# Two layers of a two-block transformer kernel: experts in pairs on float32 weights, four state-space states at a time

## The chip, the cores and the metric

The kernel runs on one core of one Trainium2 chip, as one launch. The metric is the device time of one execution in microseconds; lower is better. Three runs of the kernel before gave 2289.42, 2290.0 and 2290.57 us, so their median is 2290.0 us.

## The reference

The work is a forward pass over 256 tokens of width 1024, all in float32. It has two blocks. Block one has two layers (adaLN, a conformer convolution beside a Mamba-2 scan, then a mixture of experts). Block two has four layers: forgetting attention ("fox"), a state space layer ("S5"), a pooling mixer, and fox again, each followed by a SwiGLU feed-forward ("ffn"). The change touches two places. The first is the mixture of experts of the second layer of block one: 16 experts, of which each token gets two.

```python
def expert(acc, ew):
    wg, wu, wd, cw = ew
    hid = jax.nn.silu(t @ wg) * (t @ wu)          # 1024 -> 256
    return acc + (cw[:, None] * (hid @ wd)).astype(acc.dtype), None   # 256 -> 1024
```

The second is the S5 layer, with 64 groups of 16 channels and 64 complex states each:

```python
u = (h @ w_in).astype(F32)
...
bu = jnp.einsum('gpc,bsgc->bsgp', b_bar, u_g)
...
_, states = lax.associative_scan(combine, (lam_seq, bu), axis=1)
y = jnp.einsum('gcp,bsgp->bsgc', c_mat, states).real.reshape(B, S, D_MODEL)
y = y + d.astype(F32) * u
g = jax.nn.gelu(y).astype(h.dtype)
val, gate = jnp.split(g @ w_glu, 2, axis=-1)
return val * jax.nn.sigmoid(gate)
```

## The kernel before

Tokens lie along the free dimension (256 columns), features along the 128 partitions, so a width of 1024 is eight chunks k. A scheduler of the framework orders the instructions of each engine from the order of the code, its priorities and the buffers; nothing of the order is written by hand except the steps of generators (`yield`) that the code interleaves.

**Weights.** `raw` (L61 to 64) loads 1 MB of float32 weights by one DMA on SP's queue into a ring of five buffers. `split` (L53 to 55) makes a high part on ACT (L54) and a low part on DVE (L55), both float32r; `mm3` (L48 to 51) then multiplies three times, high by high, high by low and low by high. So a matrix costs three matmuls per tile, a pass over its weights on ACT and one on DVE, and its buffer comes free when DVE's pass is done. All matmuls are recorded at L46, in `mm`.

**Experts of the second layer.** `moe1(80)` (L949) works with a capacity of 80 tokens per expert; a path behind a branch takes what overflows. `slots` (L1309) builds one-hot matrices from the routing, and `gather` selects the tokens of four experts at a time by matmul (`px`) into `gt`, split in high and low. The experts then run one after the other through `expert` (L1148), whose parts are interleaved by `expert_step`: gate and up (`gu`, 2 x 24 matmuls of 256 columns), the SwiGLU product `hid`, its transpose `ph`, and the down product (`py`, 12 matmuls of 512 columns). Experts 0 to 11 write their rows to DRAM (`yd`) by an indirect DMA on POOL (`scattered`, L1123); the last four are added in PSUM with a one-hot matrix (`added`, `parts2` L1115, `acc`), where the rows of the first twelve also come back (`yt`, added by matmuls with the identity). `tail` (L1083) adds the result to x and prepares the first fox layer.

**S5.** `s5_table` (L1982) builds the table `s5tab` of rotations ahead of ffn 0. `s5` (L2033) computes u = h w_in in eight chunks m. Each chunk holds four tiles of 128 states, and `state(m, a)` (L2041) treats one such tile on the 32 rows or columns of strip a. It makes four products `bu` into PSUM; the rotation by the table in three DVE multiplications (A at L2052, B at L2053 and L2054); two additions on POOL (Z, L2055 and L2056); two scans on DVE over 128 positions (L2060); the rotation back, A on DVE (L2062) and B twice on POOL (L2063, L2064); and nine products back into 32 columns of y. After four tiles yy (L2076) and a GELU follow. Then `linear` (L1564) multiplies by w_glu, of which some chunks are accumulated early between the states; a tuple of triples says which. All of block two takes its PSUM from one pool with eight buffers `mm` (`bank`, L1428).

The adaLN products (`adaps`) of both layers already run before the change as plain float32 matmuls on raw weights, at 32-column strips of TensorE. The lines that matter for this are the three products of an expert, and the strip slice r in `state`:

```python
self.mm(gu[:n, q], xh[:, k], wh[:, kk], k == 0 and q == 0, False)
self.mm(gu[:n, q], xh[:, k], wl[:, kk], False, False)
self.mm(gu[:n, q], xl[:, k], wh[:, kk], False, k == KC - 1)
...
self.mm(y[r, 1], bc[:, odd, r], v, False, n == 3)
self.mm(y[r, 0, 1:], bc[:, even, r], v[:, 0:P - 1], False, n == 3)
```

Of the kernel before, what the change touches and what calls it, by code (L numbers as in the profile page):

```python
# [29 lines left out]
class Net:  # L30
# [100 lines left out]
    def block1(self):  # L131
        nc, tc, i = self.nc, self.tc, self.i
        with ExitStack() as c1:
# [26 lines left out]
            self.moe1(80)  # L160
# [788 lines left out]
    def moe1(self, cap):  # L949
# [4 lines left out]
        NT, TC, G = T, 2, 4  # L954
        with ExitStack() as c2, ExitStack() as c3:
# [22 lines left out]
            f = tmp.tile([P, 2, KC, G * cap], F32, name="mf", tag="gt", bufs=2)  # L978
            f = f.rearrange("p a k n -> p (a k n)")[:, :KC * T].rearrange("p (k t) -> p k t", k=KC)
            gts = [tmp.tile([P, 2, KC, G * cap], F32R, name="gt", tag="gt", bufs=2)]  # L980

# [6 lines left out]
            slots = self.slots(cap, TC, r, tmp, pe)  # L988
# [14 lines left out]
            def turned(e):  # L1003

                o = tmp.tile([P, T], F32R, name=f"oht{e % 4}")
                pt = pe.tile([P, T], F32, name="pot", tag="px", bufs=3)
                es = slice(e % 4 * cap, e % 4 * cap + cap)
                for j in range(TC):
                    nc.tensor.transpose(pt[:cap, j * P:j * P + P], oh[3][:, j, es].bitcast(F32), self.ident)
                nc.scalar.activation(o[:cap], pt[:cap], AF.Copy)  # L1010
# [8 lines left out]
            def added(e):  # L1019

                wcol = self.slot[3][2][:cap, e % 4:e % 4 + 1]

                def part(m):
                    for q in range(2):
                        self.mm(acc[m], y[0][:cap, q, m * P:m * P + P], ohts[e % 4][:cap], e == 12 and q == 0 and m % 2 == 0, e == 15 and q == 1)
                y = [None]

                def put(py, q):
                    if q == 0:
                        y[0] = self.b8("yhl").rearrange("p k t -> p (k t)").rearrange("p (a d) -> p a d", a=2)  # L1030
                    if q or e == 15:
                        self.parts2(y[0], py, cap, wcol, q if e == 15 else None)
                    if q == 0:
                        return
                    if e < 15:
                        for m in range(KC):
                            part(m)
                    if e == 15:
# [3 lines left out]
            for e in range(N_EXP + 1):  # L1042
                if e < N_EXP:
                    g, n = divmod(e, G)
                    if n == 0 and g < 3:
                        onehot()
                        gts.append(tmp.tile([P, 2, KC, G * cap], F32R, name="gt", tag="gt", bufs=2))
                    if e < 12:
                        _, sidx, wcol, _, _ = self.slot[g]
                        q = slice(n, n + 1)  # L1050
                        y = tmp.tile([P, D], F32, name="y", tag="y", bufs=2)
                        put = self.scattered(y, cap, wcol[:, q], sidx[:, q], NT)
                    else:
                        put = added(e)
                    es = slice(n * cap, n * cap + cap)
                    cur = self.expert(gts[g][:, 0, :, es], gts[g][:, 1, :, es], cap, [w[e] for w in ws], tmp, pe, put)
                if e == 0:
                    next(cur)
                    self.overflowed(over, TC, NT, xh, xl, ws, tmp, pe, y,
                                    (tmp.tile([P, D], F32, name="yr", tag="y", bufs=2), *(gts[1][:, q].rearrange("p k n -> p (k n)")[:, :D] for q in range(2))))  # L1060
                if e == 13:
# [4 lines left out]
                pend = self.expert_step(cur if e < N_EXP else None, pend, e == 0)  # L1066
                if e < 12:
                    for k in (2 * n, 2 * n + 1):
                        if g < 3:
                            gather(g + 1, k)  # L1070
                if 8 <= e < 12:
                    ohts.append(turned(e))
                if e == 13:
# [8 lines left out]
                if e == 14:  # L1082
# [1134 lines left out]
```

## Time and profile before

| | value |
|---|---|
| median of three runs | 2290.0 us (2289.42 to 2290.57) |
| profiled execution, its own time | 2291.34 us |
| its span in the trace | 2289.5 us |
| mean granted TensorE clock | 0.974 of full |
| expert stage, from the branch to the first matmul of fox 0 | about 843 to 1027.6 us |
| S5 states, from the first rotation to the last yy | 1374.0 to 1511.5 us |

The profile is of one execution. Its instructions are shown by engine: PE is TensorE's matmul, PEld its weight load, DVE, ACT and POOL the vector, scalar and GpSimd engines, SP the engine whose queue starts most DMAs. A float32 matmul shows as two records, a float32r one as one. A window's row gives the busy time of each engine in a stretch, the granted clock as a share of full speed, and the busy share and rate of the DMA engines. The chain of waits follows the work that ended last back through what released it.

### The profile page before, as it was taken

To read this page: it belongs to the slowest core of one execution; us is meant where nothing else is said; L and a number is where in the kernel's file an instruction comes from. 1 tells how busy PE (TensorE), PEld (TensorE's weight loads), DVE (VectorE), ACT (ScalarE), POOL (GpSimd) and SP (SyncE) were. 2 spreads that over 40 slices of the span, in tenths; PEclk is the share of its full clock that TensorE was granted. 3 is DMA by queue.
4 is the path that set the end of the run, shared out by engine and by line. 5 is a ranking of instruction groups with operands and counts; after the bars stand their busy time and mean duration, and the time that the engine had idled before them with its cause. 6 is when DMAs were issued, how large, how long until landed. Compare 5 with 4: busy or idle time off the path is not lost.

```text
span 2289.5 us, 38513 instructions
## 1 busy us (share of the span) xinstructions
PE 2151.6 (94%) x15289; PEld 1859.9 (81%) x15291; DVE 1625.8 (71%) x2711; ACT 1153.1 (50%) x1889; POOL 496.8 (22%) x693
## 2 busy tenths in 40 slices
PE   7999895998898979989999999999999999999998
PEld 3556464887585659878899998899998999989998
DVE  4887546988797578879886666668557655767654
ACT  4224633786534558866564451035446444546444
POOL 1001203312232210012358845421001000111000
PEclk9999996999999989999999999999999999999999
DMA  7554225988233559964555652125543655435551
GB/s 291 210 187 141 100 74 190 321 301 312 92 129 130 183 186 327 325 242 128 197 194 189 205 173 82 58 91 187 203 155 102 221 185 184 137 120 170 173 203 49
DMA packets 278494, 409.09 MB, mean 179 GB/s; under 512 B 11745, under 2 KB 243169, under 8 KB 272033
## 3 DMA queue, kind: packets, MB, share of 16 engines
q1 hardware_dynamic: 268576, 380.57, 49.4%
q0 software_dynamic: 8288, 19.68, 2.4%
q10 hardware_dynamic: 1440, 6.29, 0.7%
q8 instruction: 123, 2.02, 0.4%
q14 instruction: 67, 0.54, 0.1%
HBM read 390.93 MB, written 25.53 MB: 182 GB/s over the span
## 4 chain that ended last, share of the span: by engine, by line
PE 56%; DVE 4%; ACT 1%; POOL 1%; issue 1%; DMA 0%; DVEq 0%; ACTq 0%; POOLq 0%
PE mm L46 48%; PE gu L46 4%; DVE wl L55 2%; PE py L46 2%; PE px L46 1%; ACT wh L54 0%; DVE gl L1475 0%; POOL sq L1479 0%; PE mm L1701 0%; PE acc L46 0%; PE ssq L46 0%; PE mm L1917 0%; POOL p L1693 0%; DVE x L1598 0%; ACT gh L1474 0%
## 5 line engine op out<-in xcount | busy, mean ns | idle before, releaser
L55 DVE TENSOR_TENSOR wl<-raw,wh 128x1024 fp32r<-128x1024 f32 (+2 forms) x574 | 709.0, 1244 | 244.9 <-ACT wh L54 240.3
L54 ACT ACTIVATE wh<-raw 128x1024 fp32r<-128x1024 f32 (+1 forms) x586 | 613.3, 1052 | 518.8 <-PE mm L46 274.7
L46 PE MATMUL mm<-gh,wh 128*128 128x256 f32 (+1 forms) x1744 | 496.3, 285 | 0.1
L46 PE MATMUL mm<-gh,wl 128*128 128x256 f32 (+1 forms) x1744 | 492.8, 283 | 1.9 <-DVE wl L55 1.9
L46 PE MATMUL mm<-gl,wh 128*128 128x256 f32 (+1 forms) x1744 | 492.1, 282 | 0.3 <-DVE gl L1475 0.3
L46 PEld LDWEIGHTS mm<-gh,wh 128*128 128x128 f32 (+1 forms) x1744 | 327.6, 188 | 6.5 <-issue 5.5
L46 PEld LDWEIGHTS mm<-gh,wl 128*128 128x128 f32 (+1 forms) x1744 | 327.4, 188 | 4.5 <-DVE wl L55 2.5
L46 PEld LDWEIGHTS mm<-gl,wh 128*128 128x128 f32 (+1 forms) x1744 | 327.4, 188 | 2.1 <-issue 1.1
L46 PE MATMUL gu<-wh,gt 128*128 128x256 f32 (+1 forms) x1024 | 201.6, 291 | 17.7 <-ACT gt L54 7.3
L46 PE MATMUL mm<-fh,wh 128*128 128x256 f32 x704 | 198.4, 285 | 0.5 <-DVE x L1515 0.3
L46 PE MATMUL mm<-fl,wh 128*128 128x256 f32 x704 | 198.6, 283 | 0.0
L46 PE MATMUL mm<-fh,wl 128*128 128x256 f32 x704 | 198.2, 283 | 0.0
L1479 POOL TENSOR_TENSOR sq<-sq 128x256 f32<-128x256 f32 x48 | 40.3, 840 | 650.0 <-ACT sq L1477 486.9
L46 PEld LDWEIGHTS gu<-wh,gt 128*128 128x128 f32 (+1 forms) x1024 | 153.9, 174 | 23.9 <-ACT gt L54 10.3
L46 PE MATMUL gu<-wl,gt 128*128 128x256 f32 (+1 forms) x512 | 147.5, 288 | 2.3 <-DVE wl L55 2.2
L46 PEld LDWEIGHTS mm<-fh,wh 128*128 128x128 f32 x704 | 133.6, 191 | 2.4 <-DVE x L1515 1.2
L46 PEld LDWEIGHTS mm<-fl,wh 128*128 128x128 f32 x704 | 134.7, 191 | 0.1
L46 PEld LDWEIGHTS mm<-fh,wl 128*128 128x128 f32 x704 | 134.5, 191 | 0.0
L46 PE MATMUL proj<-xh,wl 128*128 128x512 f32 (+1 forms) x320 | 116.1, 363 | 11.1 <-POOL xr L534 7.8
L46 PE MATMUL proj<-xh,wh 128*128 128x512 f32 (+1 forms) x320 | 120.3, 377 | 1.6 <-ACT wh L54 1.6
L46 PE MATMUL proj<-xl,wh 128*128 128x512 f32 (+1 forms) x320 | 115.0, 360 | 0.0
L46 PE MATMUL adaps<-raw,sc 128*32 128x512 f32 x384 | 90.5, 638 | 9.1 <-DVE sc L170 7.2
(583 smaller groups left out, 4358.8 us busy)
## 6 DMA issues: line engine op xcount, KB each, us to landing
raw<-in_ffn_w_gate_up SPq DMA_DIRECT2D x88, 1024.0 KB, 5.4
raw<-in_w_ada SPq DMA_DIRECT2D x48, 1024.0 KB, 5.0
raw<-in_ffn_w_down SPq DMA_DIRECT2D x44, 1024.0 KB, 4.8
raw<-in_w_down SPq DMA_DIRECT2D x32, 1024.0 KB, 7.2
raw<-in_w_gate SPq DMA_DIRECT2D x27, 1024.0 KB, 6.8
raw<-in_w_up SPq DMA_DIRECT2D x27, 1024.0 KB, 7.0
raw<-in_fox_w_in SPq DMA_DIRECT2D x24, 1024.0 KB, 5.2
raw<-in_w_in SPq DMA_DIRECT2D x20, 1024.0 KB, 5.3
```

The costliest lines, as they stand in the source:

```text
L46: return self.nc.tensor.matmul(out, a, b, start=start, stop=stop, skip_group_check=True)
L54: self.nc.scalar.activation(hi, src, AF.Copy)
L55: (lo_eng or self.nc.vector).tensor_tensor(lo, src, hi.bitcast(F32), op=ALU.subtract)
L1479: nc.gpsimd.tensor_tensor(sq, sq, self.sq, op=ALU.add)
```

## The change

1. `moe1` runs the experts two at a time. `pair` replaces `expert`: plain float32 matmuls on the raw weights, one expert on TensorE's output columns 0 to 63 and the other on 64 to 127, in turns. The capacity becomes 64. `gather` copies one float32 tile and `hid`, `ht` are not split either. Five more 1 MB buffers (`rawe`) stand beside the five of `raw`. Six scatters of 128 rows take the place of twelve of 80; `slots` puts the slots of two experts in the two halves of the partitions.
2. `s5` runs `states(m)`, four tiles of 128 states at once: the `bu` products of the four row strips in turns into four PSUM banks, A and B as one DVE multiplication of 1024 columns each, Z as two POOL additions of 512, two scans of 512 columns (`rtab` holds the decay at each position and zero at the first of each tile), A and B back as two DVE multiplications of 1024, and the products of y in turns over the four column strips. `rtab` is filled in `s5_table` by one ACT operation of 4096 columns. The plan of `linear` no longer accumulates chunk 3 early.
3. Block two opens its PSUM pool anew for the stages, with four `mm` buffers in S5 instead of eight.

```diff
-            self.moe1(80)
+            self.moe1()
...
+            def load(w, a, n):
+
+                loaded[0] += 1
+                if loaded[0] % 10 < 5:
+                    return self.raw(w, a, n)
+                r = tmp.tile([P, a, n], F32, name="rawe", tag="rawe", bufs=5)
+                nc.sync.dma_start(r, w)
+                return r
...
-                self.split(gts[g][:, 0, k], gts[g][:, 1, k], px)
...
+                if k % 2:
+                    nc.vector.tensor_copy(gts[g][:, k], px)
+                else:
+                    nc.scalar.activation(gts[g][:, k], px, AF.Copy)
...
-            for e in range(N_EXP + 1):
...
+            for p in range(N_EXP // 2 + 1):
...
+    def pair(self, x, ws, load, tmp, pe, put):
+
+        nc = self.nc
+        half = lambda e: slice(64 * e, 64 * e + 64)
+        gu = pe.tile([P, 2, 256], F32, name="gu", tag="gu", bufs=2)
+        for q in range(2):
+            r = [load(w[q], KC, 256) for w in ws]
+            for k in range(KC):
+                for e in range(2):
+                    self.mm(gu[half(e), q], x[:, k, half(e)], r[e][:, k], k == 0 and q == 0, k == KC - 1)
+            if q == 0:
+                yield
...
+        r = [load(w[2], 2, D) for w in ws]
+        py = pe.tile([P, 2, 512], F32, name="py", bufs=1)
+        for q in range(2):
+            for f in range(2):
+                for e in range(2):
+                    self.mm(py[half(e), q], ht[:, f, half(e)], r[e][:, f, 512 * q:512 * q + 512], f == 0, f == 1)
+            put(py, q)
...
+        self.rtab = sp.tile([P, NS, P], F32, name="s5rt")
+        nc.scalar.activation(self.rtab, self.s5r[:, :, None].to_broadcast([P, NS, P]), AF.Copy)
+        nc.gpsimd.memset(self.rtab[:, :, 0:1], 0.0)
...
+            for j in range(2):
+                for q in range(2):
+                    for a in range(4):
+                        self.mm(bu[:, a, q], bc[strip(a), 2 * j + q], u[strip(a), j], j == 0 and q == 0, j == 1)
...
+            A, B, Z = t("A", four), t("B", four), t("Z", four, 1)
             nc.vector.tensor_tensor(A, bu, tab, op=ALU.mult)
-            nc.vector.tensor_tensor(B[:, 0], bu[:, 0], tab[:, 1], op=ALU.mult)
-            nc.vector.tensor_tensor(B[:, 1], bu[:, 1], tab[:, 0], op=ALU.mult)
+            nc.vector.tensor_tensor(B, bu, tab[:, ::-1], op=ALU.mult)
...
-            nc.gpsimd.tensor_tensor(B[:, 0], Z[:, 0], tab[:, 1], op=ALU.mult)
-            nc.gpsimd.tensor_tensor(B[:, 1], Z[:, 1], tab[:, 0], op=ALU.mult)
+            nc.vector.tensor_tensor(B, Z, tab[:, ::-1], op=ALU.mult)
...
+            for n, (v, q, odd, even) in enumerate(((A, 0, 4, 6), (A, 1, 9, 10), (B, 0, 5, 7), (B, 1, 5, 7))):
+                for a in range(4):
+                    self.mm(y[strip(a), 1], bc[:, odd, strip(a)], v[:, q, a], False, n == 3)
+                for a in range(4):
+                    self.mm(y[strip(a), 0, 1:], bc[:, even, strip(a)], v[:, q, a, 0:P - 1], False, n == 3)
```

Where it moves instructions, the order of an engine's rows shows it at three places. On TensorE, in the steady part of the expert stage, an expert of before reads (three products by high and low weights, out partitions x columns; `hh`, `hl` are the parts of the transposed hid):

```order
L46 MATMUL gu<-wh,gt 80x256 x2
L46 MATMUL gu<-wl,gt 80x256
L46 MATMUL gu<-wh,gt 80x256
L46 MATMUL py<-wh,hh 80x512
L46 MATMUL py<-wl,hh 80x512
L46 MATMUL py<-wh,hl 80x512
```

and a pair of the change (`raw` and `rawe` are weights as loaded):

```order
L46 MATMUL gu<-raw,gt 64x256 x17
L46 MATMUL py<-raw,ht 64x512 x8
L46 MATMUL gu<-rawe,gt 64x256
L1117 MATMUL ph<-ident,hid 128x128 x2
L46 MATMUL gu<-rawe,gt 64x256 x31
```

The split weights are gone from the rows, and a pair has 32 `gu` and 8 `py` matmuls where two experts had 96 and 24.

On SP's queue, just ahead of the branch (`cnt` is the count that the branch reads), before:

```order
L63 DMA raw<-in_w_gate 128x8x256
L63 DMA raw<-in_w_up 128x8x256
L63 DMA raw<-in_w_gate 128x8x256
L63 DMA raw<-in_w_up 128x8x256
L63 DMA raw<-in_w_down 128x2x1024
L63 DMA raw<-in_w_gate 128x8x256
L1398 DMA wd<-comb 128x2x16
L1397 DMA od<-ovri 128x2x16
L1399 TENSOR_LOAD cnt
```

and now:

```order
L63 DMA raw<-in_w_gate 128x8x256
L990 DMA rawe<-in_w_gate 128x8x256 x2
L63 DMA raw<-in_w_gate 128x8x256
L63 DMA raw<-in_w_up 128x8x256 x2
L990 DMA rawe<-in_w_up 128x8x256 x2
L1442 DMA od<-ovri 128x2x16
L1443 DMA wd<-comb 128x2x16
L990 DMA rawe<-in_w_down 128x2x1024
L1444 TENSOR_LOAD cnt
```

Nine loads now stand ahead of the branch where six stood.

On DVE, in the S5 states, one tile of 128 states before (`mm` is the PSUM tile of `bu`):

```order
L2052 TENSOR_TENSOR A<-mm,s5tab 128x256
L2053 TENSOR_TENSOR B<-mm,s5tab 128x128
L2054 TENSOR_TENSOR B<-mm,s5tab 128x128
L2060 SCALAR_TENSOR_TENSOR Z<-s5r,Z 128x128 x3
L2062 TENSOR_TENSOR A<-Z,s5tab 128x256
```

and four tiles now (the scans are the rows at L2119):

```order
L2112 TENSOR_TENSOR A<-bu,s5tab 128x1024
L2113 TENSOR_TENSOR B<-bu,s5tab 128x1024
L2119 SCALAR_TENSOR_TENSOR Z<-s5rt,Z 128x512
L2155 TENSOR_TENSOR u<-mm,rstd 128x256
L2119 SCALAR_TENSOR_TENSOR Z<-s5rt,Z 128x512
L55 TENSOR_TENSOR wl<-raw,wh 128x1024
L2121 TENSOR_TENSOR A<-Z,s5tab 128x1024
L2133 SCALAR_TENSOR_TENSOR yy<-u,cols,mm 128x2x128
L2122 TENSOR_TENSOR B<-Z,s5tab 128x1024
L55 TENSOR_TENSOR yl<-yy,yh 128x256
```

The scans and the rotation back of four tiles follow their own A and B, with one other instruction between them, and the weight split and yy of neighbouring chunks stand between the rotations.

## Rows read from the trace of the kernel before

**Rows 1.** The page, part 1: busy time of each engine, share of the span, instructions.
```profile
PE 2151.6 (94%) x15289; PEld 1859.9 (81%) x15291; DVE 1625.8 (71%) x2711; ACT 1153.1 (50%) x1889; POOL 496.8 (22%) x693
```

**Rows 2.** Windows: PE, PEld, DVE, ACT, POOL busy us (count), granted clock, DMA share, GB/s.
```profile
10.00:20.00 10.00, 6.82 (x12) 2.38 (x8) 0.00 (x0) 5.30 (x16) 0.00 (x0) 1.00 1.01 424
450.00:460.00 10.00, 9.18 (x64) 8.14 (x63) 8.61 (x10) 8.10 (x11) 3.15 (x3) 1.00 1.00 362
830.00:840.00 10.00, 7.37 (x40) 7.10 (x39) 7.89 (x47) 3.32 (x7) 0.00 (x0) 0.58 0.05 6
...
960.00:970.00 10.00, 10.00 (x76) 8.91 (x75) 8.35 (x10) 8.62 (x12) 0.91 (x2) 1.00 1.02 337
980.00:990.00 10.00, 7.75 (x49) 7.16 (x48) 6.16 (x5) 4.68 (x7) 4.21 (x3) 0.83 1.03 406
1400.00:1410.00 10.00, 10.00 (x76) 8.24 (x73) 4.82 (x14) 0.00 (x0) 5.33 (x11) 1.00 0.01 2
```

**Rows 3.** The chain of waits through one expert: start us, us, what.
```profile
932.60 2.90 PE gu L46 x24
935.50 2.76 PE py L46 x12
938.26 1.17 PE px L46 x8
```

**Rows 4.** Timeline of SP's DMA issues around the expert stage: start us, us.
```profile
817.00 0.51 SPq L63 DMA_DIRECT2D raw<-in_w_gate  x1
...
846.80 0.38 SPq L63 DMA_DIRECT2D raw<-in_w_up  x1
...
978.44 8.06 SPq L63 DMA_DIRECT2D raw<-in_w_down  x2
```

**Rows 5.** Timeline of TensorE and its weight loads in an adaLN product at strips.
```profile
808.18 8.45 PE L46 MATMUL adaps<-raw,sc 128*32 128x512 f32 x32 [0.56 <-ACT rs L290]
...
812.17 0.11 PEld L46 LDWEIGHTS adaps<-raw,sc 128*32 128x32 f32 x2 [0.32 <-issue]
```

**Rows 6.** Timeline of TensorE at the end of the expert stage.
```profile
997.78 3.73 PE L46 MATMUL acc<-ident,yt 128*128 128x128 f32 x32
...
1011.96 0.40 PE L46 MATMUL py<-wh,hh 128*80 128x512 f32 x1
...
1027.63 0.47 PE L46 MATMUL mm<-gh,wh 128*16 128x256 f32 x1
```

**Rows 7.** The chain of waits through the S5 states.
```profile
1374.04 0.43 DVE A L2052
...
1377.76 133.74 PE mm L46 x1004
1511.53 0.49 DVE yy L2076
```

**Rows 8.** Groups of DVE instructions by shape: count | busy us, mean ns | idle before.
```profile
L55 DVE TENSOR_TENSOR wl<-raw,wh 128x1024 fp32r<-128x1024 f32 x568 | 705.8, 1251 | 243.9 <-ACT wh L54 239.4
...
L2060 DVE TENSOR_TENSOR_SCAN Z<-s5r,Z 128x128 f32<-128x128 f32 x64 | 35.1, 580 | 1.4 <-POOL Z L2056 1.4
L2062 DVE TENSOR_TENSOR A<-Z,s5tab 128x256 f32<-128x256 f32 x32 | 17.7, 553 | 0.1
...
L1619 DVE TENSOR_TENSOR_SCAN negc<-ones,f 16x256 f32<-16x256 f32 x2 | 1.4, 675 | 0.0
```

**Rows 9.** Groups of POOL instructions by shape.
```profile
L2055 POOL TENSOR_TENSOR Z<-A 128x128 f32<-128x128 f32 x32 | 15.4, 480 | 65.7 <-DVE A L2052 65.7
L1081 POOL TENSOR_TENSOR yt<-yt 128x512 f32<-128x512 f32 x4 | 8.1, 2056 | 15.2 <-DMA yt<-yd 15.1
```

**Rows 10.** Timeline of ACT at the start of ffn 0.
```profile
1173.42 1.28 ACT L1459 ACT_TABLE_LOAD   x1
...
1175.34 4.11 ACT L54 ACTIVATE wh<-raw 128x1024 fp32r<-128x1024 f32 x4
```

**Rows 11.** Waits of TensorE from 1160 to 1200 us: us in total, times, longest.
```profile
PE mm L46 <- DVE wl L55: 0.2, 1, 0.2
```

More of the change, by code (lines that the diff above doesn't have):

```diff
@@ L1065, in moe1 @@
                     acc = [banks[m // 2][:, m % 2] for m in range(KC)]
[L1066 to L1073, printed above, removed]
+                pend = self.expert_step(cur if p < N_EXP // 2 else None, pend, p == 0)
+                if p < 6:
+                    for k in range(4 * n, 4 * n + 4):
+                        gather(g + 1, k)
+                if 4 <= p < 6:
+                    ohts.append(turned(n))
+                if p == 6:
                     y = self.yd.rearrange("(j p k) d -> j p k d", p=P, k=2)
@@ L1405, in block2, with banks @@
             self.tmp = c1.enter_context(tc.tile_pool(name="tmp2", bufs=1))
-            self.pm = c1.enter_context(tc.tile_pool(name="pm2", bufs=1, space=PSUM, reuse_waits="tile"))
-            with tc.high_priority(offset=-400):
-                self.enter2()
-            with tc.tile_pool(name="s5p", bufs=1) as self.sp:
-                steps = self.s5_setup()
-                def aside(n=3):
-                    with tc.high_priority(offset=-100):
-                        for _ in range(n):
-                            next(steps, None)
-                self.fox(0, self.V["ffn"][0], aside)
-                aside(1000)
+            def banks(n=8):
+                self.nbank = n
+                return tc.tile_pool(name="pm2", bufs=1, space=PSUM, reuse_waits="tile")
@@ new lines, in block2, with aside @@
+            with banks() as self.pm:
+                with tc.high_priority(offset=-400):
+                    self.enter2()
+                with tc.tile_pool(name="s5p", bufs=1) as self.sp:
+                    steps = self.s5_setup()
+                    def aside(n=3):
+                        with tc.high_priority(offset=-100):
+                            for _ in range(n):
+                                next(steps, None)
+                    self.fox(0, self.V["ffn"][0], aside)
+                    aside(1000)
@@ L1424, in block2 @@
-            self.ffn(2, self.V["mix"][3])
-            self.fox(1, self.V["ffn"][3])
-            self.last()
+            with banks() as self.pm:
+                self.pool_layer(lambda each, aside: self.ffn(1, None, each=each, aside=aside), self.V["mix"][2], self.V["ffn"][2])
+                self.ffn(2, self.V["mix"][3])
+                self.fox(1, self.V["ffn"][3])
+                self.last()
     def bank(self, shape, dt=F32):
-        return self.pm.tile(shape, dt, name="mm", tag="mm", bufs=8)
+        return self.pm.tile(shape, dt, name="mm", tag="mm", bufs=self.nbank)
@@ L2080, in turn @@
+            yy = t("yy", [P, T])
+            nc.vector.scalar_tensor_tensor(halves(yy), u, self.V["d"][:, m:m + 1], y, op0=ALU.mult, op1=ALU.add)
+            nc.scalar.activation(yy, yy, AF.Gelu_apprx_tanh)
+            self.split(yh[:, m], yl[:, m], yy)
         def turn(*new):
-            live[:] = [g for g in [*new, *live] if next(g, self) is not self]
+            live[:] = [g for g in [*live, *new] if next(g, self) is not self]
         raw = None
```

152 lines of the change are left out of this document (74 added, 78 removed).

## The prediction

> **What bounds the kernel now.** I read the page first, then windows over the two changed stages, then the chain of waits inside each, then single rows for prices. The page shows TensorE busy for 94% of the span [rows 1], so time can only come from stages where it does less work afterwards. In the expert stage TensorE is busy 10.00 of 10 us at full clock, and the DMA engines are full beside it, in 960:970, share 1.02 at 337 GB/s [rows 2]. So two limits nearly touch there. The chain of one expert is matmuls alone: 24 for gate, 24 for up at 2.83 to 2.90 us each, 2.76 us down, 1.17 us of gather [rows 3], 9.7 us with the transposes. In the S5 states TensorE is also busy 10.00 of 10, while the DMA engines do nothing (share 0.01) and DVE works 4.8 of 10, in 1400:1410 [rows 2]. The chain there is one piece of 133.74 us of matmuls, from the first rotation at 1374.04 to the last yy at 1511.53 [rows 7]. So in S5 only TensorE matters, and DVE and POOL have room.
>
> **The change part by part.** *Do strips overlap?* The price of both parts hangs on this. A float32 matmul leaves two records; the identity products take 3.73 us for 32 records of 128 columns, 0.117 us each, one after the other [rows 6]. By that, a record of 512 columns alone would take some 0.43 us or more, and the 32 records of an adaLN product 14 us. They take 8.45 us with their waits, and their weight loads come as x2, two per step, with a step of 0.43 us (0.11 busy and 0.32 idle) [rows 5]. So two strips run side by side: a round of both is 0.43 us for 256 columns and 0.86 us for 512. I carry this from 32 columns to 64, which the trace does not show.
>
> *Experts, TensorE.* A pair then needs 16 rounds of 0.43 for gate and up (6.9), 4 of 0.86 for down (3.4) and 16 gather matmuls of 256 columns at 2.90/24 = 0.12 (1.9), together 12.2 us, where two experts took 19.3.
>
> *Experts, DMA.* The six loads of a pair, 6.3 MB, take 18.7 us at 337 GB/s, more than 12.2. So the stage becomes bound by its loads, and what counts is when the last one lands. Before, buffers were full at the branch and the queue stood still from 817.00 to 846.80 [rows 4]. The change has nine loads issued there, by five more buffers; I count from 843.4, where the branch is left. Remaining are 39 loads of 1.0486 MB (40.9 MB), the return of yt (2.1 MB), and 348 scattered rows of 4 KB (1.4 MB): 44.4 MB. The stage's own rate is 337, and the same kind of loads made 362 at share 1.00 in 450:460 [rows 2]. I take 350 between them: 127 us, last load at L = 970. At 337 it is 975, at 362 it is 966. After L, the products of the seventh pair are added (L + 2.6), the 32 identity records take 3.73 us (L + 6.3), and then stands what stood from the last py to fox, 1011.96 to 1027.63 = 15.7 [rows 6], with 0.6 for a longer py. Fox begins at L + 22.6 = 992.6 instead of 1027.6: **-35 us** (-30 at 337, -39 at 362). That ACT and DVE no longer split weights costs nothing and gains nothing here; they were beside TensorE. Splits freed the buffers before; now matmuls do.
>
> The Trainium skill puts the limit of HBM for one core at about 358 GB/s (DMA: Bandwidth & Descriptors, Specifications); by it L would come 3 us earlier. The trace agrees only in part: 362 in one window, but 424 and 406 at shares 1.01 and 1.03 in others [rows 2].
>
> *S5, TensorE.* Per four tiles: w_in 24 matmuls at 0.118 (2.8); `bu`, 32 records on four strips, 8 rounds at 0.117 (0.9); y, 72 records on four strips, 18 rounds (2.1, up to 2.6). That is 6 to 6.6 us, where the whole took 133.74/8 = 16.7. So another engine takes over.
>
> *S5, DVE and POOL.* A, B, A and B again are four operations of 1024 columns; the nearest row is a DVE operation of that size, 1.25 us [rows 8]. (L2062's 0.553 for 256 columns would give 2.2; but POOL multiplied beside it, and that work is gone.) A scan of 512 columns: 16x256 took 0.675 [rows 8], so about 1.25; four times the 0.580 of 128 columns is the other end, 2.3. POOL's Z of 512 columns is 4 x 0.480 = 1.9 or the 2.06 of its row [rows 9]. In the order on DVE: A and B to 2.5 us; POOL's two Z end at 3.2 and 5.2; so the scans end at 4.5 and 6.5 with u between them; then a weight split 1.25, A 1.25, yy 0.5 [rows 7], B 1.25, yl 0.5 gives 11.2. I take **11.5 us a cycle**, since POOL and DVE work at once; bounds 10.5 (Z hidden) and 13.4 (slow scans). Eight cycles are 92 us; the last has no successor to split for (-3.2), then y 2.6, and 1.7 for constant operations of the pool layer that the order puts ahead of the last yy: 93 us from 1374, so yy at 1467 instead of 1511.5, -44.5. The plan that accumulates less in advance leaves 21 matmuls at 0.118 for later, +2.5. S5: **-42 us** (-27 to -50). POOL's two B multiplications move to DVE, off POOL's path, and are in the sum.
>
> *The table of decays.* One ACT operation of 4096 columns, four times a weight split (4.11 for four of 1024 [rows 10]), now stands ahead of the table load, rstd and the first weight splits of ffn 0. There TensorE waits only 0.2 us for splits in 40 us [rows 11], so little cover is left: **+4 us** (0 if the ring of split weights covers it, 6 with what queues behind it).
>
> *Clock and PSUM.* Where TensorE waits, the granted clock falls: 0.58 in 830:840 after the routing's waits, 0.83 in 980:990 [rows 2]. I put **+2 us** (0 to 6) for slow stretches on the path, in the two tails and at the start of S5's matrix product. Four PSUM buffers instead of eight cost nothing as long as DVE is the bound; if not, they are in the 13.4.
>
> **Sum.** -35 - 42 + 4 + 2 = -71. The profiled execution took 2291.3, so 2220.3; it lay 1.3 above the median of 2290.0, hence **2219 us**.
>
> **The rivals.** *Loads run faster* than in the stage before, as in 980:990 with 406 GB/s. The stage before may have held DMA back at 337 because TensorE freed buffers no faster; its share of 1.02 speaks against it, since the engines were not idle. Then L = 953, the experts give -52, and the time is 2202.
>
> *TensorE at half clock.* Both stages leave it waiting a third to a half of the time. By the clock seen after waits (0.58 in 830:840 [rows 2]) the 12.2 us of a pair become up to 21; with half of the work slow, 18.3 us, eight pairs end at 990, the tail's 18 us follow, and fox comes at 1008 (-20). S5's cycle, with slow y products on its path, is then 13.4 (-27). Sum -41: 2249. For it: 980:990 stays at 0.83 with 7.75 us busy. Against it: ten buffers let TensorE work in long stretches.
>
> The Trainium skill names this mechanism too: an array that pauses falls to 1.2 GHz and has to earn 2.4 GHz back (TensorE: Matmul & The Clock Gate, Part 1). The trace agrees as far as the 0.58 above shows.
>
> *Slower:* strips of 64 columns do not overlap. A pair then takes 32 x 0.43 + 8 x 0.86 + 1.9 = 22.5 us instead of 19.3, the stage ends about 16 us later, and if S5's strips fail too it gains nothing and pays 2.5; with 4 for the table the time is about 2312. It decides once a round of two 64-column strips costs over some 0.7 us. The rows on adaLN speak against it, for 32 columns outright.
>
> *The change doesn't act*, because an expert overflows its 64 tokens and the branch is taken, or the gains are hidden: about 2290. The inputs give the fullest expert 62 tokens, so I leave almost nothing for it.
>
> **How the numbers follow.** My forecast has a chance of 0.61, faster loads 0.12, half clock 0.20, no overlap 0.05, no change 0.02. A measurement of this kernel can tell 0.2%, some 5 us, from no change; only the last two cases are not faster by that much. So faster 0.93, same 0.02, slower 0.05. The range goes from the faster loads with S5's 10.5 us cycle (2202 - 8) to the half clock's upper edge: **2193 to 2251**. It leaves out the no-overlap case and the outer parts of the others.
>
> **What would show it.** Right: in the middle of the expert stage TensorE busy 6 to 8 of 10 with a DMA share near 1.0; `gu` rounds of two records per 0.22 us; the first fox matmul near 993; in S5 DVE busy over 8 of 10 and TensorE near 6; the last yy 93 us after the first A; a wait of TensorE for `wh` at the start of ffn 0 of some 4 us. Wrong: a granted clock near 0.6 through these stages, a DMA share clearly under 1 with TensorE waiting for loads, POOL's Z well over 2 us, or waits of SP for buffers that only late matmuls free.

## The result and the profile after

The changed kernel takes **2207.3 us** (median of 4 runs, 2206.05 to 2207.91), against 2290.28 us for the kernel before beside it: a ratio of 0.9635, 95% interval 0.9619 to 0.9652. That is 83 us faster; 71 were forecast, and the time lies inside the range of 2193 to 2251. The profiled execution of the change took 2206.05 us with a span of 2204.3.

The page of the kernel after, part 1, against [rows 1]:

```profile
PE 2029.2 (92%) x14919; PEld 1719.2 (78%) x14919; DVE 1485.5 (67%) x2437; ACT 1039.6 (47%) x1744; POOL 440.6 (20%) x576
```

TensorE lost 122 us of work and the span 85, so TensorE now waits 37 us more. Windows of the kernel after show where (columns as in [rows 2]). The first two are from the expert stage, the third is all of it, the fourth the S5 states, the last the 8 us behind them:

```profile
870.00:880.00 10.00, 10.00 (x72) 5.82 (x70) 1.27 (x3) 1.77 (x3) 0.98 (x1) 1.00 1.06 381
910.00:920.00 10.00, 7.00 (x45) 3.31 (x46) 0.42 (x1) 0.38 (x1) 0.00 (x0) 1.00 1.06 374
...
840.00:955.00 115.00, 101.68 (x732) 59.32 (x727) 13.91 (x52) 17.83 (x32) 5.85 (x6) 0.96 1.06 367
...
1336.20:1421.00 84.80, 61.63 (x999) 53.81 (x998) 82.37 (x92) 15.27 (x31) 23.64 (x32) 0.86 0.26 82
...
1424.00:1432.00 8.00, 7.46 (x36) 6.87 (x36) 6.32 (x11) 5.85 (x9) 0.17 (x1) 0.54 0.41 133
```

In the expert stage the DMA engines are full from end to end, share 1.06 at 367 GB/s; TensorE lives on the loads that were ahead, and its chain of waits has the first piece of DMA at 905.49 us. In the states DVE is busy 82.37 of 84.80 us and TensorE 61.63. So both stages changed their bound, as forecast: to the loads, and to DVE.

To compare, I cut both traces at the same five instructions: the first matmul of fox 0, the table load ahead of ffn 0's rstd, the first A of S5, the last yy, the end. The before column uses [rows 6, 7, 10].

| stretch | before | after | difference | forecast |
|---|---|---|---|---|
| start to fox 0 | 1027.63 | 983.65 | -44.0 | -35 |
| fox 0 to table load of ffn 0 | 145.8 | 153.4 | +7.6 | +4, to the first A |
| table load to first A | 200.6 | 199.2 | -1.4 | |
| first A to last yy | 137.5 | 84.6 | -52.9 | -44.5 |
| last yy to end | 778.0 | 783.5 | +5.5 | +2.5 |
| span | 2289.5 | 2204.3 | -85.2 | -71 with +2 for the clock |

The timeline of TensorE in the kernel after, in a pair and at the end of the stage (start us, us, what):

```profile
875.10 3.67 PE L46 MATMUL gu<-rawe,gt 128*64 128x256 f32 x30
...
955.70 3.65 PE L46 MATMUL py<-rawe,ht 128*64 128x512 f32 x14
...
963.38 3.73 PE L46 MATMUL acc<-ident,yt 128*128 128x128 f32 x32
967.04 1.94 PE L46 MATMUL py<-rawe,ht 128*64 128x512 f32 x8
...
983.65 0.47 PE L46 MATMUL mm<-gh,wh 128*16 128x256 f32 x1
```

Thirty records of 256 columns take 3.67 us, 0.12 each, half of what the pace of the identity products [rows 6] gives for one after the other: two strips side by side, as the adaLN rows had it [rows 5]. The tail is the one of before: from the last py (967.04) to fox 16.6 us, against 15.7 + 0.6 in the forecast.

The timeline of DVE in the states of the kernel after, one cycle (in square brackets the idle time before and its releaser):

```profile
1386.55 1.22 DVE L2112 TENSOR_TENSOR A<-bu,s5tab 128x1024 f32<-128x1024 f32 x1
...
1396.97 1.22 DVE L2112 TENSOR_TENSOR A<-bu,s5tab 128x1024 f32<-128x1024 f32 x1
1398.10 1.21 DVE L2113 TENSOR_TENSOR B<-bu,s5tab 128x1024 f32<-128x1024 f32 x1
1399.63 2.27 DVE L2119 TENSOR_TENSOR_SCAN Z<-s5rt,Z 128x512 f32<-128x512 f32 x1 [0.32 <-POOL Z L2114]
1401.82 0.45 DVE L2133 SCALAR_TENSOR_TENSOR yy<-u,cols,mm 128x256 f32<-128x256 f32 x1
1402.19 1.22 DVE L2119 TENSOR_TENSOR_SCAN Z<-s5rt,Z 128x512 f32<-128x512 f32 x1
1403.44 1.23 DVE L2121 TENSOR_TENSOR A<-Z,s5tab 128x1024 f32<-128x1024 f32 x1
```

and POOL beside it:

```profile
1398.33 1.27 POOL L2114 TENSOR_TENSOR Z<-A 128x512 f32<-128x512 f32 x1 [7.92 <-DVE A L2112]
1399.56 1.26 POOL L2115 TENSOR_TENSOR Z<-B 128x512 f32<-128x512 f32 x1
```

This cycle, A to A, is 10.4 us (1386.55 to 1396.97), the longest kind; the seven cycles of the stage take 9.1 to 10.4 us, 10.0 on average (1336.24 to 1406.06). Two things stand out: the first scan takes 2.27 us where the second takes 1.22, just while POOL's second Z runs; and POOL's first Z, beside B, slows nothing.

### The profile page after: what moved, and what is told of

The parts are those of the page before. It is cut to its first block, busy times and chain, and to the rows that moved or that the text cites. A ratio compares the mean times of both kernels' runs of the same rounds, so it can differ in the third digit from the quotient of the medians.

```text
span 2204.3 us, 37044 instructions
## 1 busy us (share of the span) xinstructions
PE 2029.2 (92%) x14919; PEld 1719.2 (78%) x14919; DVE 1485.5 (67%) x2437; ACT 1039.6 (47%) x1744; POOL 440.6 (20%) x576
## 4 chain that ended last, share of the span: by engine, by line
PE 48%; DVE 8%; DMA 2%; ACT 1%; issue 1%; POOL 1%; SPq 0%; DVEq 0%; POOLq 0%; ACTq 0%
PE mm L46 43%; DVE wl L55 2%; PE gu L46 2%; PE py L46 1%; DVE Z L2119 1%; DMA rawe<-in_w_down 1%; PE px L46 1%; DVE gl L1525 1%; DMA rawe<-in_w_up 1%; DMA raw<-in_w_down 1%; DVE A L2112 0%; PE mm L1751 0%; DVE A L2121 0%; POOL Z L2114 0%; ACT wh L54 0%
## 5 line engine op out<-in xcount | busy, mean ns | idle before, releaser
L55 DVE TENSOR_TENSOR wl<-raw,wh 128x1024 fp32r<-128x1024 f32 (+2 forms) x478 | 592.5, 1244 | 234.5 <-ACT wh L54 232.6
L54 ACT ACTIVATE wh<-raw 128x1024 fp32r<-128x1024 f32 x490 | 512.9, 1050 | 495.9 <-PE mm L46 268.5
L46 PE MATMUL proj<-xh,wl 128*128 128x512 f32 (+1 forms) x320 | 118.0, 369 | 10.2 <-POOL xr L534 6.9
L46 PE MATMUL gu<-wh,gt 128*128 128x256 f32 x512 | 101.6, 295 | 16.3 <-ACT gt L54 7.3
L46 PEld LDWEIGHTS gu<-wh,gt 128*128 128x128 f32 x512 | 83.0, 196 | 22.0 <-ACT gt L54 10.3
L46 PEld LDWEIGHTS proj<-xh,wh 128*128 128x128 f32 x320 | 63.1, 197 | 42.8 <-issue 29.8
```

Source lines behind the costliest of these rows:

```text
L46: return self.nc.tensor.matmul(out, a, b, start=start, stop=stop, skip_group_check=True)
L54: self.nc.scalar.activation(hi, src, AF.Copy)
L55: (lo_eng or self.nc.vector).tensor_tensor(lo, src, hi.bitcast(F32), op=ALU.subtract)
```

## The experiments

All kernels ran beside the kernel before; its medians there were 2291.7, 2292.1 and 2292.7 us, and ratios refer to those.

### The parts alone

**Experts alone** is the change with `s5`, `s5_table` and the PSUM pools as before; **S5 alone** is the kernel before with those three changed.

> The paired experts alone, with the S5 layer as before. In the trace of the change fox 0 starts 44.0 us earlier than before, and nothing of S5 stands ahead of it. Theory (the two parts act on separate stages and add up): 2290 - 44 = 2246 us, fox 0 near 984. Rival (part of the gain comes from the rest of the change, by an earlier start of the stage, or the tail of the stage gives some back later): the 35 us of the prediction, 2255 us, or less.

> The S5 part alone, with the experts as before. From the trace of the change: fox 0 and ffn 0 6.2 us longer, the states 52.8 us shorter, the rest 5.4 us longer, together -41: 2249 us. If the two parts help or hinder each other, this and the run of the experts alone will not add up to the 83 us of both.

Measured: experts alone 2247.17 us, ratio 0.9796 (0.9777 to 0.9814), fox 0 at 984.48; S5 alone 2255.61 us, ratio 0.9831 (0.9814 to 0.9849), with +7.6 us from fox 0 to the first A, -52.9 in the states and +7.4 behind them. The first came out as the theory said. The second is nearly 7 us above it; in its trace 3.9 of these stand ahead of fox 0, in code that is as before. Runs of the kernel before spread by 7 us (2289.32 to 2296.52) on that chip, so I don't read more into it. The parts add up to 80.6 us, the change gave 83: the gains are separate, with no interaction that can be told.

### What bounds the expert stage

Three kernels differ from the change only in `pair` or `load`. **Strips in blocks**: all matmuls of one expert, then all of the other.

```diff
-            for k in range(KC):
-                for e in range(2):
+            for e in range(2):
+                for k in range(KC):
                     self.mm(gu[half(e), q], x[:, k, half(e)], r[e][:, k], k == 0 and q == 0, k == KC - 1)
...
-            for f in range(2):
-                for e in range(2):
+            for e in range(2):
+                for f in range(2):
```

> The change, but in a pair all matmuls of one expert come before those of the other, so the two 64-column strips no longer take turns; same matmuls, loads and bytes. Theory (two strips run side by side only when their matmuls alternate): a pair on TensorE goes from 12.2 to 16 x 0.86 + 8 x 0.86 + 1.9 = 22.6 us, above the 17 us of its loads; eight pairs become bound by TensorE, some 50 to 60 us more: 2255 to 2267 us, gu at one record per 0.21 us. Rival (strips of 64 columns gain nothing from taking turns, and the records only look overlapped): 2207 us, as the change.

Measured: 2227.55 us, ratio 0.9713 (0.9697 to 0.9729), fox 0 at 1003.05, so 19.4 us later. Neither number was right. The timeline of TensorE in this kernel:

```profile
955.78 0.64 PE L46 MATMUL py<-rawe,ht 128*64 128x512 f32 x1
955.99 0.59 PE L46 MATMUL gu<-rawe,gt 128*64 128x256 f32 x2
...
956.64 0.59 PE L46 MATMUL py<-raw,ht 128*64 128x512 f32 x1
956.69 0.59 PE L46 MATMUL py<-rawe,ht 128*64 128x512 f32 x1
957.07 0.59 PE L46 MATMUL py<-raw,ht 128*64 128x512 f32 x1
```

and its chain of waits through one pair (start us, us, what):

```profile
850.49 5.81 PE gu L46 x30
856.67 5.60 PE gu L46 x29
862.70 3.65 PE py L46 x15
```

The blocks of gate and up, 16 records per expert, went from some 3.6 us to 5.6 to 5.8: taking turns is what pays. But that is 1.6 times, not twice, and the down product, in blocks of 4 records, nearly keeps its pace (3.65 us here for 15 records, 3.43 for 16 in the same view of the change). The rows suggest why: records of the other strip start while the first strip's are still under way, though they come later in the order of the code (here a `py` product starts between records of `gu`, and the `py` products on `raw` and `rawe`, one expert each, alternate). So a pair takes about 17 us on TensorE (2 x 5.7 + 3.65 + 1.9), just the pace of its loads (6.3 MB at 367 GB/s). Eight such pairs are 136 us of matmuls, while part of the loads had run ahead of the branch. So TensorE became the bound: it is busy without a gap from 840 to 970 us, and over 840 to 955 the DMA engines fell to a share of 0.97 at 329 GB/s.

**A third of the loads left out**: the up product multiplies by the gate weights again.

```diff
-            r = [load(w[q], KC, 256) for w in ws]
+            r = r if q else [load(w[q], KC, 256) for w in ws]
```

> The change, but the up product uses the gate weights again, so 16 of the 48 loads of 1 MB are left out; the matmuls are the same in number and shape. Theory (the stage is bound by its loads): 28 MB instead of 44 take 76 us, less than TensorE's 8 x 12.2 = 98; so the stage ends bound by TensorE, 20 to 25 us earlier: about 2184 us, with a DMA share clearly under 1. Rival (TensorE or the hand-over between matmuls and loads sets the pace): within 5 us of 2207.

Measured: 2187.6 us (2 runs), fox 0 at 964.21, 19.4 us earlier. The window over the stage in this kernel:

```profile
840.00:935.00 95.00, 95.00 (x724) 57.18 (x722) 16.09 (x50) 19.04 (x33) 5.87 (x6) 1.00 0.84 292
```

TensorE is busy throughout and DMA is not: without the 16 loads the bound goes back to TensorE, as the theory said. So the loads cost the change's stage about 19 us beyond what TensorE needs.

**Five buffers**: all weights through `raw`, no `rawe`.

```diff
-                if loaded[0] % 10 < 5:
-                    return self.raw(w, a, n)
+                return self.raw(w, a, n)
```

> The change with the five buffers of before for all weights of the pairs (no rawe), so at most five loads are under way or waiting to be used. Theory (the stage is bound by its loads, and they keep going only while a buffer is free): fewer loads are done ahead of the branch (five instead of nine, 4 x 2.87 = 11.5 us more to load after it), and of the six loads of a pair at most five fit, so the queue stands still while matmuls hold buffers: 10 to 25 us more, 2217 to 2232 us, with a DMA share clearly under 1 in the stage. Rival (ring depth doesn't matter once matmuls free the buffers): within 4 us of 2207.

Measured: 2228.13 us (2222.8 to 2233.18), ratio 0.9712 (0.9692 to 0.9732), fox 0 at 1007.37 in the trace, 23.7 us later. That is within the theory's range, though the DMA share over the stage fell only to 1.00 at 349 GB/s; half of the loss is then the loads that no longer run ahead of the branch (4 x 2.87 = 11.5). The rest is slower loading, some 6 us by the two rates, and a tail at a lower clock, some 4 us (the `py` ahead of the sums take 6.49 us instead of 3.65, at a granted clock of 0.59 in 975 to 982). The queue did stand for buffers, as the theory has it: from 840 to 985 us SP waited 78.0 us for `gu` products and 28.4 for `py`, which free the buffers, against 26.9 and 9.7 in the change. The trace is of the longest of the four runs (2233.18 us). By the medians, 21 of the 44 us of the experts, about half, hang on the five extra buffers.

### The table of decays

The timeline of ACT in the change, ahead of ffn 0:

```profile
1129.42 0.40 ACT L1527 ACTIVATE sq<-x 128x256 f32<-128x256 f32 x1
1133.39 3.63 ACT L2040 ACTIVATE s5rt<-s5r 128x4096 f32<-128x4096 f32 x1 [3.58 <-DMA bcd<-s5m]
1137.04 1.28 ACT L1509 ACT_TABLE_LOAD   x1
```

and the waits of TensorE there, 1115 to 1160 us (us in total, times, longest):

```profile
PE mm L46 <- ACT wh L54: 2.1, 1, 2.1
PE mm L46 <- DVE wl L55: 1.6, 2, 1.4
PE mm L46 <- ACT fh L54: 1.4, 1, 1.4
```

The operation itself is 3.63 us, but ahead of it ACT stands still for 3.58 us: the row names the DMA that stores `bcd` from `s5m`, and everything behind, rstd and the weight splits, stands behind both. The experiment fills the table in eight pieces of 512 columns during ffn 0, each pinned in ACT's order:

```diff
-        nc.scalar.activation(self.rtab, self.s5r[:, :, None].to_broadcast([P, NS, P]), AF.Copy)
-        nc.gpsimd.memset(self.rtab[:, :, 0:1], 0.0)
+        def decays():
+            for s in range(0, NS, 4):
+                yield
+                yield
+                self.tc.keep_in_program_order(nc.scalar.activation(self.rtab[:, s:s + 4], self.s5r[:, s:s + 4, None].to_broadcast([P, 4, P]), AF.Copy))
+                nc.gpsimd.memset(self.rtab[:, s:s + 4, 0:1], 0.0)
+        self.decays = decays()
...
-                    self.ffn(0, self.V["mix"][1])
+                    self.ffn(0, self.V["mix"][1], aside=lambda: next(self.decays, None))
+                    for _ in self.decays:
+                        pass
```

> The change, with the table of decays filled in eight pieces of 512 columns during ffn 0 instead of one of 4096 columns ahead of it. From fox 0 to the table load of ffn 0 before took 145.8 us and the change 153.4; ACT stands 3.58 us waiting for the DMA that stores bcd and then 3.63 us in the operation. Theory (both are on the path, for rstd and the weight splits queue behind them on ACT): 145.8 again, 5 to 7 us less, about 2201 us. Rival (the waits of ffn 0 come from the half clock or the splits, and ACT's operation only stands in idle time): no more than 2 us.

Measured: 2200.15 us (2199.56 to 2200.89), ratio 0.9598 (0.9585 to 0.9611), 7 us below the change. From fox 0 to the table load it takes 148.4 us, and to the first A 345.8 instead of 352.6. The same waits of TensorE, 1110 to 1160 us, in this kernel:

```profile
PE mm L46 <- DVE wl L55: 1.0, 2, 0.8
PE mm L46 <- DVE x L1650: 0.4, 1, 0.4
PE mm L46 <- ACT wh L54: 0.3, 1, 0.3
```

The theory holds: from fox 0 to the first A the time is that of the kernel before (346.4 us). The experiment removes the wait and the long operation together, so it does not tell the two apart.

### The constants ahead of the last yy

The timeline of DVE in the change, at the end of the states:

```profile
1414.86 0.42 DVE L55 TENSOR_TENSOR yl<-yy,yh 128x256 fp32r<-128x256 f32 x1
1415.19 0.16 DVE L1780 TENSOR_TENSOR pbs<-cols 128x8 f32<-128x8 f32 x1
...
1420.83 0.47 DVE L2133 SCALAR_TENSOR_TENSOR yy<-u,cols,mm 128x256 f32<-128x256 f32 x1
```

and of TensorE beside it:

```profile
1414.99 1.08 PE L46 MATMUL mm<-B,bc 128*32 128x128 f32 x32
...
1422.26 1.01 PE L46 MATMUL mm<-yh,wh 128*128 128x256 f32 x3 [4.56 <-ACT yh L54]
```

The last products of y are done by 1416.07, but yy starts 4.8 us later, behind 5.6 us of constants of the pooling layer that nobody needs yet; TensorE, which had some products of w_glu until 1417.7, then stands still for 4.56 us and comes back at a granted clock near 0.54 (1424 to 1432), about the lower level of 1.2 GHz. The experiment adds a dependency of order, for each of these DVE operations on the last yy:

```diff
-            nc.vector.scalar_tensor_tensor(halves(yy), u, self.V["d"][:, m:m + 1], y, op0=ALU.mult, op1=ALU.add)
+            self.yylast = nc.vector.scalar_tensor_tensor(halves(yy), u, self.V["d"][:, m:m + 1], y, op0=ALU.mult, op1=ALU.add)
...
+                    ins = getattr(nc.vector, n)(*a, **k)
+                    tc.add_manual_dep(ins.ins, last.ins.name, mybir.DependencyInfo(mybir.DependencyClass.NoSync, mybir.DependencyReason.DATA), reason="behind yy")
```

> The change, with the pool layer's constant operations on DVE ordered behind the last yy. In the trace of the change the products of the last y end near 1417, but yy starts at 1420.83, behind 5.6 us of those constants, and TensorE idles 4.56 us and restarts at half clock until 1432. Theory: yy starts some 4.5 us earlier, the wait of TensorE falls to 1.5 us, and some of the half clock's cost goes too: last yy about 80 us after the first A (84.6), 5 to 9 us in all, 2198 to 2202 us. Rival (the constants are needed anyway and only come back as a wait later, at the weight splits of the glu): within 2 us of 2207.

Measured: 2202.22 us (2199.96 to 2211.71), ratio 0.9614 (0.9594 to 0.9635), which overlaps that of the change. In the trace the last yy comes 79.9 us after the first A instead of 84.6, as expected; the clock still sinks later (0.66 in 1424 to 1428), and the stretch behind yy is 784.8 instead of 783.5. So the 4.7 us are shown where they were taken out; it is not shown that they reach the end in full.

### DVE and POOL in the states

Two kernels move work between the engines, in opposite directions. **The second Z on DVE**, ahead of both scans (a dependency of order holds them back):

```diff
-            nc.gpsimd.tensor_tensor(Z[:, 1], B[:, 1], B[:, 0], op=ALU.subtract)
+            z1 = nc.vector.tensor_tensor(Z[:, 1], B[:, 1], B[:, 0], op=ALU.subtract)
```

> The change, with the second Z on DVE instead of POOL, ahead of both scans. In the trace of the change the first scan of each four takes 2.27 us while POOL's second Z (1.27) runs, the second 1.21 alone. Theory (a DVE operation with both operands in SBUF and a POOL operation exclude each other, so POOL's 1.27 us is paid on DVE anyway): the first scan falls to 1.2, the added Z costs about 0.6, a cycle falls from 10.4 to 9.6 us, states 6 to 7 us shorter, 2200 us. Rival (DVE is simply the busiest engine, and the long scan waits for its input): 8 x 0.6 = 5 us longer, 2212 us.

**Half of the second B on POOL**:

```diff
-            nc.vector.tensor_tensor(B, Z, tab[:, ::-1], op=ALU.mult)
+            nc.vector.tensor_tensor(B[:, 0], Z[:, 0], tab[:, 1], op=ALU.mult)
+            nc.gpsimd.tensor_tensor(B[:, 1], Z[:, 1], tab[:, 0], op=ALU.mult)
```

> The change, with half of the second B (512 of 1024 columns) on POOL, which is idle 74% of the states, instead of DVE. Theory (exclusion of DVE and POOL, as above): DVE saves 0.57 us and loses about POOL's 1.3 us while both want SBUF, a cycle 0.3 to 0.8 us longer, 2210 to 2214 us. Rival (DVE bound, POOL free): 8 x 0.57 = 4.6 us shorter, 2202 us.

Measured: with Z on DVE 2201.38 us (2198.83 to 2202.99), ratio 0.9604 (0.9590 to 0.9617), states 76.2 us instead of 84.6, so 8.4 shorter with more work on the busiest engine. Not all of it is the edit's: the seven cycles are 4.7 us shorter (65.1 instead of 69.8), the last one another 0.8, and 2.9 come from fewer constants ahead of the last yy (2.7 instead of 5.6 us, by the order of the instructions). With half of B on POOL 2215.04 us, ratio 0.9667 (0.9652 to 0.9682), which just touches the interval of the change; states 89.8 us, 5.2 longer with less work on DVE, of which 3.6 are in the seven cycles and 1.6 are more constants. Groups of DVE instructions by shape, 1345 to 1410 us, in the first:

```profile
L2119 DVE TENSOR_TENSOR_SCAN Z<-s5rt,Z 128x512 f32<-128x512 f32 x14 | 16.6, 1211 | 0.0
...
L2115 DVE TENSOR_TENSOR Z<-B 128x512 f32<-128x512 f32 x7 | 4.8, 682 | 0.0
```

and in the second:

```profile
L2121 DVE TENSOR_TENSOR A<-Z,s5tab 128x1024 f32<-128x1024 f32 x6 | 13.4, 2225 | 0.0
...
L2113 DVE TENSOR_TENSOR B<-bu,s5tab 128x1024 f32<-128x1024 f32 x6 | 7.3, 1209 | 0.0
```

In the first all scans take 1.21 us; in the second A from Z, now beside POOL's B, takes 2.23 instead of 1.22, while B from `bu`, which reads PSUM and stands beside POOL's first Z, stays at 1.21. Once in the second kernel the order put another DVE operation beside POOL's B (1409.98 to 1411.54 us), and A behind it:

```profile
1410.34 1.48 DVE L55 TENSOR_TENSOR yl<-yy,yh 128x256 fp32r<-128x256 f32 x1
1411.74 1.21 DVE L2121 TENSOR_TENSOR A<-Z,s5tab 128x1024 f32<-128x1024 f32 x1
```

There the low part of yy, 0.41 us elsewhere, pays, and the same A does not. In all these rows POOL's time is paid on DVE where the DVE operation takes both its operands from SBUF. By the cycles the theory holds both ways, and the rival falls both ways.

### The three edits together, and POOL out of the states

**Three edits** is the change with the table in pieces, the constants behind yy and the second Z on DVE. **Both Z on DVE** moves the first Z there too:

```diff
-            nc.gpsimd.tensor_tensor(Z[:, 0], A[:, 0], A[:, 1], op=ALU.add)
+            nc.vector.tensor_tensor(Z[:, 0], A[:, 0], A[:, 1], op=ALU.add)
```

> The change with the three edits together: the pool layer's constants behind the last yy, the table of decays in pieces during ffn 0, the second Z on DVE. Theory (three separate places on the path, whose gains add up): by the segments of the traces -4.7 for yy, -6.8 for the table, -6.9 (8.4 less what the constants took) for the cycle, about 17 us less than 2207: 2190 us, states near 72 us. Rival (the gains overlap, since TensorE becomes the bound of the states near 6.6 us a cycle or the weights of the glu come late): 2196 us or more.

> As the kernel with the three edits, but the first Z is on DVE too, and POOL does nothing in the states. Theory (DVE and POOL exclude each other only where the DVE operation has no operand in PSUM; the first Z stood beside B, which reads PSUM, at no cost): 8 x 0.6 = 5 us longer than with the three edits. Rival (any work on POOL costs DVE its own time): the same or shorter.

Measured: three edits 2194.94 us (2188.79 to 2197.56), ratio **0.9574** (0.9557 to 0.9590), the fastest of all complete kernels and below the change's interval of 0.9619 to 0.9652. The states are 74.6 us and fox 0 to the first A 346.2. The profiled execution has a span of 2189.7, 14.6 below the change, while the median is only 12 below, with a spread of 9 us between runs; the 17 of the theory were not reached. The states are 10.0 us shorter, not 11.6. That is no loss between the gains: of the second Z's 8.4 us above, 2.9 were constants, which the first edit removes anyway, and the theory took off only 1.5. With 5.5 for the second Z the sum of 4.7 + 5.5 is 10.2. From fox 0 to the first A the gain is 6.4 of the 6.8 us, and 2.2 us more than in the change stand ahead of fox 0, in code that is the same.

With both Z on DVE it is 2200.01 us, ratio 0.9600 (0.9585 to 0.9614), 5 us more, as expected, with states of 81.9 us (+7.3); the two intervals overlap. But these 7.3 us are not the price of the moved Z. The timelines of TensorE and of DVE at the end of its states:

```profile
1407.16 1.83 PE L46 MATMUL mm<-B,bc 128*32 128x128 f32 x30
...
1412.55 0.41 PE L46 MATMUL mm<-B,bc 128*32 128x127 f32 x2
```

```profile
1412.99 0.48 DVE L2151 SCALAR_TENSOR_TENSOR yy<-u,cols,mm 128x256 f32<-128x256 f32 x1 [4.18 <-PE mm L46]
```

The last two records of y stand behind products of w_glu in TensorE's order, and yy waits 4.18 us for them. Of the 7.3 us 5.7 lie behind the last A, and the seven cycles are only 1.5 us longer (66.6 instead of 65.1), with two weight splits moved out of them. What the moved Z costs is read from its rows, 0.60 us from start to start (1391.30, 1391.90, 1392.50), 4.8 us in eight cycles; and that POOL's first Z was free is read from B beside it, 1.21 us in the change and 1.24 here, where POOL does nothing. So the time agrees with the theory, but does not prove it by itself.

## Why the prediction was right, and where it was off

**The two bounds.** Both stages changed to the bound that was named, loads and DVE; leaving out loads showed the first, and moving single operations on and off DVE the second. That strips of 64 columns overlap, taken over from 32, holds; the rival without overlap falls with the 3.67 us per 30 records. What the smaller capacity and the wider scatters give by themselves was not tried.

**Experts, -35 forecast, -44.0 measured.** The sum's mechanism was right, and its sizes were each a little off. The last weight load (issued at 942.52, under way for 20.5 us) landed at 963.0 instead of 970, and fox 0 followed 20.6 us later instead of 22.6: the seventh pair's products were added while that load was still under way. So 2 of the 9 us are the tail. Of the 7 us of loading some 3.5 are the rate. It was taken as 350 GB/s between 337 and 362 [rows 2]; windows of the stage before and of the loading after:

```profile
850.00:970.00 120.00, 120.00 (x886) 107.66 (x885) 105.45 (x142) 102.54 (x138) 10.35 (x12) 1.00 0.96 324
```

```profile
839.60:963.00 123.40, 108.03 (x764) 62.55 (x760) 16.12 (x57) 19.34 (x33) 10.84 (x10) 0.96 1.06 368
```

The loading took 123.4 us instead of 127 (with loads of the next stage, which already ran at its end). The mistake was to read the share of 1.02 at 337 as the limit of the engines. In the stage before, TensorE paced the loads, and the DMA engines were 0.96 busy; with loads always queued the share rose to 1.06, and the rate with it. So the rival of faster loads was half right: 368, not 406. The figure of 358 GB/s for one core from the Trainium skill (DMA: Bandwidth & Descriptors, Specifications) lies below what this core moved for 115 us; here the measurement decides.

The other 3.8 us are the start of the loading, 839.6 instead of 843.4, a term I did not have. The first gather matmul stands at

```profile
832.85 0.60 PE L46 MATMUL px<-ohr,th 128*128 128x320 f32 x1 [0.97 <-DVE ohr L1335]
```

before, and after at

```profile
828.21 0.55 PE L46 MATMUL px<-ohr,th 128*128 128x256 f32 x1 [0.91 <-DVE ohr L1379]
```

In all eleven kernels that run experts in pairs it stands at 826.8 to 829.2, and with S5 alone at 834.5, so the gain belongs to the experts. Before, weight splits of the first expert stood among the router's own splits, three on ACT (at 802.45, 803.72 and 819.65, 1.05 us each) and three on DVE (3.7 us), and they are gone; that this makes all of the 3.8 us is argued, not tried.

The standstill of the queue from 817.00 to 846.80 [rows 4] was put down to full buffers alone. But SP, which issues the loads in order, waited there 16.0 us for DVE's `comb`, which a store ahead of the branch needs, and 4.8 us for `cnt`; only 3.1 us are a wait of the next load behind the branch. In the change it stood in the same way from 831.63 to 839.61, 4.0 us of it for `cnt`, and the tenth load went out at once behind the branch. So near the branch the order of SP's queue holds loads back as well as the ring does; no run here moves it.

**S5 states, -44.5 forecast, -52.9 measured.** The terms were too high: the cycles were 9.1 to 10.4 us, 10.0 on average, not 11.5. POOL's Z of 512 columns took 1.27 us, not 1.9 to 2.06, and whole DVE operations 1.14 us from start to start. Even the bound of 10.5 was a little high. But the reason that I gave for 11.5, that POOL and DVE work at once, was right in kind: it stands as 1.06 us in the first scan of each cycle, and the move of the second Z to DVE showed it.

**The constants ahead of yy** were forecast at 1.7 us; the row shows 5.6 of them, and 4.8 between the end of the products and yy. This is part of the 84.6: from the last A to the last yy it took 14.8 us, where the sum has 12.6, so the seven cycles alone gained 10.7 us against the forecast.

**The table of decays, +4 forecast, +7.6 to the table load, +6.2 to the first A.** The operation was sized right (3.63 us), but ahead of it ACT waits for a DMA, 3.58 us, that I did not look for: as I read the row, the new tile lies in memory of a pool just closed (`s5p`) and waits for that pool's last reader. It came out at the upper end of its bounds (6), for a reason that the bounds did not contain.

**The clock, +2 forecast.** In the 8 us behind the states at 0.54, 36 matmuls came 0.21 us apart where 0.12 is their pace after 1432; by my estimate that cost some 3 us of TensorE's work, and 2.5 us of work moved into that stretch are another part of its +5.5. In the expert stage the clock held 0.96 on average, so the half-clock rival falls there. (That rival was also priced wrongly: half of 12.2 us at 0.58 gives 16.6 us a pair, not 18.3, and the loads would have stayed the bound.) In the states it was granted 0.86, and did not count, since DVE was the bound. That four PSUM buffers cost nothing fits DVE being busy 82.37 of 84.80 us, but was not tried by itself.

**The sum** was -71 against -85 of span: 9 from the experts, 8 from S5, less 3 from the table and the clock. Both large terms were sized with too little gain: the loads took their price from rows in which they were paced by another engine, POOL's Z from an addition that took 2.06 us in another place or from four small ones, and the DVE operations from their length instead of the step from one start to the next.

## What to carry to other kernels

When a stage loses its bound, price the next one from what it does when it is never kept waiting: a DMA share near 1 beside a busy TensorE was not the limit of the queue here. When work is moved to DVE or POOL, count their operations as one engine's wherever the DVE operand pair lies in SBUF, place POOL's work beside DVE operations that read PSUM, and compare cycles, since the end of a stage can shift by an order of instructions that nobody chose. And when an operation is put ahead of a stage, look at what its tile waits for and at what queues behind it on its engine, not at its own duration alone.

## What the runs showed of the hardware

- A DVE scan of 512 columns takes 1.21 us alone and 2.27 beside a POOL addition of 1.27; a multiplication of 1024 columns from SBUF 1.22 alone and 2.23 beside a POOL multiplication of 1.59. A multiplication of 1024 columns with one operand in PSUM takes 1.21 beside POOL's addition. The Trainium skill has it that POOL shares its SBUF interfaces with DVE instructions that have two SBUF inputs (GPSIMD Engine Reference, 1. Specifications); the trace agrees, and gives the price: DVE loses most of the time in which the two stand side by side, 1.06 us of 1.19 for the scan (1399.63 to 1400.82).
- Float32 matmuls on two 64-column strips overlap fully in turns (0.12 us per record of 256 columns), and in part when they come in blocks: 5.6 to 5.8 us instead of 3.6 for two blocks of 16 records, and 3.65 instead of 3.43 for blocks of 4.
- The DMA engines moved 367 GB/s over 115 us at a share of 1.06, where [rows 2] had 337 at 1.02.
